# Feed-forward block order, later settling of the down projection, and attention multiplies on VectorE in a hybrid encoder layer

## The chip, the cores and the metric

The kernel runs on one core of one Trainium2 chip. The metric is the device time of one execution in microseconds (us); the kernel before has a median of 1443.12 us over three runs (1441.78 to 1444.57).

## What is computed

One layer on x of 1024 positions by 1024 channels, float32. Cut to what matters here:

```python
h = rmsnorm(x, norm_mix_pre)
conv_in, q, k, v, g_conv, g_att = split(h @ w_in)
u = glu(conv_in); u = causal_depthwise_conv(u, 31 taps); u = silu(layernorm(u))
conv_out = u @ w_conv_branch + b
# stick-breaking attention, 8 heads of 64, strictly causal, in blocks of 128 queries:
#   a[t, s] = sigmoid(z[t, s]) * prod over s < r < t of sigmoid(-z[t, r])
att_out = attention(q, k, v) @ w_att_branch
merged = sigmoid(g_conv) * conv_out + sigmoid(g_att) * att_out
x = x + rmsnorm(merged @ w_out, norm_mix_post)
gate, up = split(rmsnorm(x, norm_ffn_pre) @ w_ffn_up)        # 2 x 2816 columns
x = x + rmsnorm((silu(gate) * up) @ w_ffn_down, norm_ffn_post)
```

## The kernel before, in words

**Precision by halves.** Every matrix is held as a high part (rounded, type float32r) and a low part (what is left). ScalarE copies the high part, and VectorE or GpSimd subtracts it from the source for the low part. A product is three matmuls: high by high, high by low, low by high (`mm3`, L76). A helper `load_w` (L66) loads a weight block, and its subtraction runs on the engine that `low_of` names (L64, GpSimd until L436, then VectorE).

**Who sets the order.** Up to L1103 a scheduler orders each engine's instructions by their place in the program and by when their tiles' slots come free. From L1103 on, each engine keeps the program's order (`Ordered`, L935): what stands first in the program is first in the engine's queue, and a waiting instruction holds what is behind it. SyncE issues all loads and stores of that part in order.

**Start and attention** (L148 to L428). Eight blocks of 128 rows are normalised (`pre`, L166; the scale by the row's root is L177, the root's power is GpSimd's, L107), transposed and split, and v is projected. Then come 8 heads, each in 4 steps of two query blocks. For each block of scores (`chunk`, L237) TensorE makes z, ScalarE the sigmoids of -z and z, VectorE a product scan from the right (L257 for the diagonal part, L262 for a full chunk of 512 columns), and the scan is multiplied by the sigmoid of z: on VectorE for the diagonal part (L259), on GpSimd for a full chunk (L263). `weigh` (L307) transposes the result on TensorE, splits it, and multiplies by v. Projections of later heads and of the conv branch fill TensorE in between; their weights come through `load_w`.

**Output projection** (L683 to L845). For each of 8 row blocks `tb`: `out_steps`, `post` (norm, residual, second norm) and `operands(tb - 2)` (transposes, and the sums that the feed-forward wants). The first two of the eight output weights sit in slots of the pool `wst` that the feed-forward's gate weights (`fetch_gate` L807, `prep_a` L811) use later.

**Feed-forward up** (L943 to L1042). 22 column blocks `f`. Each is a 2 by 2 block product done with seven products instead of eight (numbers 1 to 7, `product` L916), of 12 matmuls each, on operands T1 to T4 and B11, B21, B22 and on sums of the gate and up weights. Products 1 and 2 of blocks 0 to 2 are made early (L839). Within a block, 1 and 2 give u2 and gate1; 6 is added to u2, 7 gives u3, 5 makes up2 and the new u2, then 3 gives the second gate and 4 the first up half. Block 0 is special, since T4 is computed on VectorE in its middle (`make_t4`, L920), and so is the last one, where B22 has to come free. Each product has one of eight PSUM banks. For the next block, `sums_12` and `split_12` make the weights of products 5 and 6, `sums_34` and `split_34` those of 7 and 3, `prep_c` that of 4; `weight_sums` makes sums of the down weights. Activations and their pair sums (`quads`, L1029) go to DRAM by way of the list `late`, which `flush` (L861) empties into SyncE's queue.

**Feed-forward down** (L1056 to L1204). The same seven-product scheme in the order 1, 6, 7, 5, 4, 2, 3 (L1067), each product over 6 steps of two of the 11 column groups (the last step has one): 42 steps in all. `fetch(n)` loads both operands of step n, `ready(n)` splits them (two copies on ScalarE, two subtractions on VectorE, L1083), `cell(n, p, bank)` does piece p of 4, 6 matmuls (3 in the half step that ends each product), and `evacuate(i, p, bank)` takes a finished piece from PSUM (L1156). For products 4 and 2/3 that includes `square` (ScalarE), `gained` (times the gain, on GpSimd or VectorE) and `finish` (L1149: root, then two scaled sums with x1 and the stores). `x1_of` (L1144) loads x1 into one of two buffers. The loop:

```python
for n, (i, gs) in enumerate(work_list):
    fetch(n + AHEAD + 2); flush()
    ready(n + AHEAD)                 # AHEAD = 3
    if i == order[-1]: continue
    for p in range(4):
        cell(n, p, banks[p])
        if gs[-1] == NG - 1: evacuate(i, p, banks[p])
for p in range(4):                   # the last product, piece by piece
    for n in range(N - len(steps), N): cell(n, p, banks[p])
    evacuate(order[-1], p, banks[p]); flush()
```

## Time and profile before

| what | value |
|---|---|
| median of three runs | 1443.12 us (1441.78 to 1444.57) |
| the profiled execution, its own time | 1447.73 us |
| its span, first to last instruction | 1445.9 us |
| TensorE matmuls, busy | 1371.8 us (95%), 6412 |
| VectorE busy | 1044.4 us (72%), 1509 instructions |
| ScalarE busy | 529.2 us (37%) |
| GpSimd busy | 169.8 us (12%) |
| mean granted TensorE clock | 0.983 |

PE is TensorE, PEld its weight loads, DVE VectorE, ACT ScalarE, POOL GpSimd, SPq SyncE's queue. In a timeline a row gives start, duration, engine, line and operation; a bracket at its end says how long the engine sat idle before it and what ended that. From L1103 on all instructions carry the line of the ordering helper, L941, so they are told apart by their tiles: md is a bank of the down projection, m one of the up projection, wl and wh are low and high parts. A matmul's duration overlaps the next one's; what counts is the distance between starts. The granted clock is 1.00 at the upper of the two levels (2.4 GHz) and 0.5 at the lower (1.2 GHz).

### The profile page before, as it was taken

The numbers are of one execution on the slowest core, as the hardware profiler recorded it, in microseconds if no ns is written. First come the engines' busy times: TensorE is split into PE (matmuls) and PEld (weight loads), VectorE is DVE, ScalarE is ACT, GpSimd is POOL, SyncE is SP. The second block draws the span as 40 slices with busy tenths as digits, with TensorE's granted clock in tenths as the row PEclk, the third lists the DMA queues.
The fourth block names the chain that finished last, engine by engine and source line by source line (L and its number), as shares of the span: only waits on it lengthen the run. The fifth ranks groups of instructions, "written<-read, shape, count | busy, mean of one in ns | idle before, by whom it ended". The sixth has DMA issues, their size and how long they took to land.

```text
span 1445.9 us, 17263 instructions
## 1 busy us (share of the span) xinstructions
PE 1371.8 (95%) x6412; PEld 1127.8 (78%) x6412; DVE 1044.4 (72%) x1509; ACT 529.2 (37%) x863; POOL 169.8 (12%) x259
## 2 busy tenths in 40 slices
PE   6988899999999999999997899999999998999987
PEld 5866787777787888888886688888888887888866
DVE  5498887865999967236559889888888775644573
ACT  5466655554111126132335233222222222632350
POOL 2133333331000000000126000000000000000220
PEclk9999999999999999999998999999999999999998
DMA  6011010100102021114322344444444435964272
GB/s 224 23 26 41 9 37 30 45 29 15 51 22 69 27 88 37 51 44 158 126 87 74 124 168 167 167 167 168 157 163 145 147 131 207 374 226 160 103 262 102
DMA packets 62403, 160.97 MB, mean 111 GB/s; under 512 B 6384, under 2 KB 17904, under 8 KB 62320
## 3 DMA queue, kind: packets, MB, share of 16 engines
q1 hardware_dynamic: 62032, 158.83, 32.1%
q8 instruction: 50, 0.82, 0.2%
q10 hardware_dynamic: 288, 1.05, 0.2%
q14 instruction: 33, 0.27, 0.1%
HBM read 117.65 MB, written 40.11 MB: 109 GB/s over the span
## 4 chain that ended last, share of the span: by engine, by line
PE 72%; DVE 18%; issue 3%; ACT 3%; DMA 1%; POOL 1%; SPq 0%; DVEq 0%; POOLq 0%; ACTq 0%
PE m L941 28%; PE md L941 12%; DVE p L469 7%; PE pg L82 3%; PE pg L79 3%; PE pg L80 3%; PE po L697 2%; PE po L695 2%; PE po L696 2%; DVE R L262 2%; PE pb L82 1%; DVE R L257 1%; PE pb L79 1%; PE pb L80 1%; PE av L293 1%
## 5 line engine op out<-in xcount | busy, mean ns | idle before, releaser
L941 PE MATMUL m<-t,wh 128*128 128x512 f32 x528 | 134.9, 397 | 4.4 <-ACT wh L941 3.0
L941 PE MATMUL m<-hH,wh 128*128 128x512 f32 x328 | 130.6, 398 | 8.9 <-ACT wh L803 8.9
L941 PE MATMUL md<-wl,wh 128*128 128x512 f32 x308 | 123.3, 400 | 9.7 <-DVE wl L941 9.7
L941 PE MATMUL m<-hL,wh 128*128 128x512 f32 x328 | 130.1, 397 | 0.0
L941 PEld LDWEIGHTS m<-t,wh 128*128 128x128 f32 x528 | 100.0, 190 | 29.0 <-ACT wh L941 3.4
L941 PE MATMUL md<-wh 128*128 128x512 f32 x308 | 122.4, 398 | 0.0
L941 ACT ACTIVATE c<-c 128x512 f32<-128x512 f32 x44 | 27.9, 634 | 244.9 <-DVE c L941 244.9
L72 ACT ACTIVATE wh<-wraw 128x1024 fp32r<-128x1024 f32 (+1 forms) x60 | 56.5, 946 | 124.7 <-PE pg L80 30.2
L79 PE MATMUL pg<-hH,wh 128*128 128x512 f32 x256 | 100.7, 393 | 0.0
L80 PE MATMUL pg<-hL,wh 128*128 128x512 f32 x256 | 99.7, 389 | 0.0
L941 PE MATMUL md<-wh,wl 128*128 128x512 f32 x308 | 99.3, 397 | 0.0
L941 PE MATMUL m<-hH,wl 128*128 128x512 f32 x328 | 89.2, 393 | 0.0
L73 DVE TENSOR_TENSOR wl<-wraw,wh 128x1024 fp32r<-128x1024 f32 (+1 forms) x45 | 46.7, 1049 | 48.5 <-ACT wh L72 36.7
L941 PEld LDWEIGHTS m<-hH,wh 128*128 128x128 f32 x328 | 62.2, 190 | 23.8 <-ACT wh L803 9.3
L469 DVE SCALAR_TENSOR_TENSOR p<-u,dw,p 128x513 f32<-128x513 f32 (+1 forms) x116 | 80.2, 789 | 0.0
L941 PEld LDWEIGHTS md<-wl,wh 128*128 128x128 f32 x308 | 59.3, 193 | 24.7 <-DVE wl L941 11.8
L941 DVE TENSOR_TENSOR wl<-ra,wh 128x1024 fp32r<-128x1024 f32 (+1 forms) x42 | 48.5, 1154 | 37.9 <-ACT wh L941 37.8
L941 PEld LDWEIGHTS m<-hL,wh 128*128 128x128 f32 x328 | 62.2, 190 | 14.0
L941 PEld LDWEIGHTS m<-hH,wl 128*128 128x128 f32 x328 | 61.7, 188 | 14.4
L941 PE MATMUL m<-t,wl 128*128 128x512 f32 x264 | 70.7, 390 | 0.0
L941 DVE TENSOR_TENSOR u<-m,u 128x512 f32<-128x512 f32 x66 | 45.4, 688 | 33.8 <-PE m L941 32.1
L941 PEld LDWEIGHTS md<-wh 128*128 128x128 f32 x308 | 59.3, 193 | 12.8 <-ACT wh L941 0.3
(235 smaller groups left out, 3326.3 us busy)
## 6 DMA issues: line engine op xcount, KB each, us to landing
ra<-act SPq DMA_DIRECT2D x35, 512.0 KB, 7.1
wraw<-in_wi SPq DMA_DIRECT2D x32, 512.0 KB, 3.5
rg<-in_wu SPq DMA_DIRECT2D x23, 512.0 KB, 4.5
ru<-in_wu SPq DMA_DIRECT2D x22, 512.0 KB, 5.5
q<-in_wdq SPq DMA_DIRECT2D x22, 512.0 KB, 6.3
wsum<-q SPq DMA_DIRECT2D x22, 512.0 KB, 2.6
act<-sa SPq DMA_DIRECT2D x44, 256.0 KB, 2.7
rb<-wsum SPq DMA_DIRECT2D x20, 512.0 KB, 9.6
```

Of the source, the lines that this page charges most:

```text
L72: A.activation(out=wh, in_=raw, func=AF.Copy)
L73: (sub or low_of[0]).tensor_tensor(out=wl, in0=raw, in1=wh.bitcast(F32), op=ALU.subtract)
L79: PE.matmul(ps, lhsT=lh, rhs=rh, start=(first and j == 0), stop=False)
L80: PE.matmul(ps, lhsT=lh, rhs=rl, start=False, stop=False)
L82: PE.matmul(ps, lhsT=ll, rhs=rh, start=False, stop=(last and j == n - 1))
L257: V.tensor_tensor_scan(out=R[:, 3:3 + n][:, ::-1], data0=d, data1=d, initial=1.0, op0=ALU.mult, op1=ALU.bypass)
L262: V.tensor_tensor_scan(out=R[:, 4:4 + n][:, ::-1], data0=d, data1=d, initial=carry, op0=ALU.mult, op1=ALU.bypass)
L469: V.scalar_tensor_tensor(out=to if last is None else last, in0=u[:, k:k + n], scalar=w, in1=to, op0=ALU.mult, op1=ALU.add)
L695: PE.matmul(pb, lhsT=hH[:, d, tsl], rhs=wos[d][0][:, es], start=(d == 0), stop=False)
L696: PE.matmul(pb, lhsT=hL[:, d, tsl], rhs=wos[d][0][:, es], start=False, stop=False)
L697: PE.matmul(pb, lhsT=hH[:, d, tsl], rhs=wos[d][1][:, es], start=False, stop=(d == NK - 1))
L941: return lambda *a, **k: tc.keep_in_program_order(fn(*a, **k))
```

## The change

Seven edits. `low_of` starts with VectorE. The multiply of a full chunk (L263) goes from GpSimd to VectorE. The fetch and split of the gate weights of blocks 0 and 1 stand three row blocks earlier in the program. Block 0 and the last block of the feed-forward up run product 5 before 3; in block 0 all of T4 is made before product 6 and the next block's first sums and split stand right behind it, with the other sums further down; in the last block `ready(0)` stands before product 6. The pair sums of the last block are put off until `ready(1)` has been issued. In the down projection a finished product's pieces are evacuated one step later, behind the next `ready`; product 4's `gained` runs on VectorE and its `finish` one piece later; and the last product runs its pieces 0 and 1 step by step like the other products, pieces 2 and 3 one after the other.

```diff
-    low_of = [G]
+    low_of = [V]
...
-            G.tensor_tensor(out=R[:, 4:4 + n], in0=sg[:, 0:n], in1=R[:, 4:4 + n], op=ALU.mult)
+            V.tensor_tensor(out=R[:, 4:4 + n], in0=sg[:, 0:n], in1=R[:, 4:4 + n], op=ALU.mult)
...
-        if NT - 4 < tb < NT - 1:
-            f = tb - NT + 3
-            fetch_gate(f)
-            prep_a(f)
+        if tb < 4:
+            fetch_gate(tb - 2)
+            prep_a(tb - 2)
...
         if f == 0 or last:
+            run(5)
             run(3)
-            run(5)
             if f == 0:
-                make_t4(range(2))
+                make_t4(range(4))
+            if last:
+                ready(0)
             run(6)
             after_6()
             if f == 0:
-                make_t4(range(2, 4))
+                sums_12(nf)
+                split_12(nf)
...
-        if f == 0:
-            sums_12(nf)
-            split_12(nf)
-            sums_34(nf)
-            weight_sums(f)
-        if last:
-            ready(0)
...
         V.tensor_tensor(out=a2, in0=up2, in1=gate2, op=ALU.mult)
+        if f == 0:
+            sums_34(nf)
...
             prep_c(nf)
+        if f == 0:
+            weight_sums(f)
...
+            def pair_sums():
+                s = {i: half_tile(f"sa{i}", "a", 8) for i in (5, 6, 7, 3)}
...
+            if last:
+                return pair_sums
+            pair_sums()
...
-        up(f)
+        last_sums = up(f)
...
     fetch(1)
     fetch(2)
+    ready(1)
+    last_sums()
     flush()
...
-    for n in range(1, AHEAD):
-        ready(n)
+    ready(2)
...
+    roots = {}
+
+    def root(sst):
+        return power_of(sst[:, 0:1], 1, sst[:, 1:2])
+
-    def finish(tb, parts, sst, xt):
-        r = power_of(sst[:, 0:1], 1, sst[:, 1:2])
+    def finish(tb, parts, r, xt):
...
             square(0, c21[p], sst2[p])
-            gained(0, c21[p], G)
-            finish(p + 4, (c21[p], c22[p]), sst2[p], xt)
+            gained(0, c21[p], V)
+            roots[p] = root(sst2[p]), xt
+            for q in ([p - 1] if p else []) + ([p] if p == 3 else []):
+                finish(q + 4, (c21[q], c22[q]), *roots[q])
...
-    banks = []
+    banks, done = [], []
+
+    def settle():
+        for args in done:
+            evacuate(*args)
+        done.clear()
+
+    FIRST_OF_LAST = N - len(steps)
     for n, (i, gs) in enumerate(work_list):
...
             ready(n + AHEAD)
-        if i == order[-1]:
-            continue
-        for p in range(4):
+        settle()
+        for p in range(4 if n < FIRST_OF_LAST else 2):
             cell(n, p, banks[p])
             if gs[-1] == NG - 1:
-                evacuate(i, p, banks[p])
-    for p in range(4):
-        for n in range(N - len(steps), N):
+                done.append((i, p, banks[p]))
+    for p in (2, 3):
+        for n in range(FIRST_OF_LAST, N):
             cell(n, p, banks[p])
-        evacuate(order[-1], p, banks[p])
+        settle()
         flush()
+        done.append((order[-1], p, banks[p]))
+    settle()
+    flush()
```

## Rows read from the trace of the kernel before

**Rows 1.** Busy time in 20 us stretches: us, engines' busy us (instructions), granted clock, DMA, GB/s
```profile
80.00:100.00 20.00, 15.72 (x93) 12.59 (x93) 19.58 (x34) 12.36 (x28) 8.55 (x19) 1.00 0.00 1
...
740.00:760.00 20.00, 20.00 (x95) 16.37 (x93) 12.88 (x17) 8.82 (x17) 7.73 (x6) 1.00 0.33 107
```

**Rows 2.** Timeline of the start, VectorE and TensorE: start us, us, engine, line, operation
```profile
26.12 3.38 DVE L177 SCALAR_TENSOR_TENSOR xt<-xt,pr,gpre 128x1024 f32<-128x1024 f32 x1 [1.04 <-POOL pr L107]
...
30.89 1.28 DVE L177 SCALAR_TENSOR_TENSOR xt<-xt,pr,gpre 128x1024 f32<-128x1024 f32 x1 [0.73 <-POOL pr L107]
...
29.64 1.06 PE L115 MATMUL tp<-ident,xt 128*128 128x128 f32 x8 [2.64 <-DVE xt L177]
```

**Rows 3.** Groups by line and shape, attention: count, busy us, mean ns, idle before
```profile
L263 POOL TENSOR_TENSOR R<-sg,R 128x512 f32<-128x512 f32 x32 | 46.7, 1461 | 78.2 <-DVE R L262 74.8 <-PE tpa L317 1.8 <-ACT aH L322 1.6
...
L73 POOL TENSOR_TENSOR wl<-wraw,wh 128x1024 fp32r<-128x1024 f32 x15 | 37.0, 2469 | 62.1 <-ACT wh L72 57.5 <-issue 4.6
...
L73 DVE TENSOR_TENSOR wl<-wraw,wh 128x1024 fp32r<-128x1024 f32 x29 | 35.8, 1238 | 48.5 <-ACT wh L72 36.7 <-PE pg L82 11.2 <-issue 0.4
...
L259 DVE TENSOR_TENSOR R<-sg,R 128x511 f32<-128x511 f32 x16 | 14.9, 933 | 0.6
...
L259 DVE TENSOR_TENSOR R<-sg,R 128x255 f32<-128x255 f32 x16 | 13.4, 839 | 0.9
```

**Rows 4.** Timeline, VectorE: the same multiply alone and beside a GpSimd multiply
```profile
65.81 0.42 DVE L259 TENSOR_TENSOR R<-sg,R 128x255 f32<-128x255 f32 x1
...
80.11 1.23 DVE L259 TENSOR_TENSOR R<-sg,R 128x255 f32<-128x255 f32 x1
```

**Rows 5.** Chain that ended last, 60 to 365 us, shares by line (cut short by the view)
```profile
by line: DVE R L262 7.7%; issue 7.1%; DVE R L257 6.2%; PE av L293 5.3%; PE tpa L317 5.3%; DVE aL L323 5.1%; PE av L292 4.8%; PE psg L82 4.2%; DVE R L259 3.7%; PE psg L80 3.7%; PE psg L79 3.5%; PE z L245 3.0%; PE psq L82 3.0%; PE psk L82 2.9
```

**Rows 6.** Timeline of the feed-forward's first block, ScalarE, VectorE and TensorE
```profile
786.50 1.06 ACT L803 ACTIVATE wh<-s 128x1024 fp32r<-128x1024 f32 x1 [1.24 <-DVE s L896]
790.92 1.06 ACT L803 ACTIVATE wh<-rg 128x1024 fp32r<-128x1024 f32 x1 [3.36 <-DVE rg L901]
...
791.41 0.68 DVE L941 TENSOR_TENSOR da<-t,hH 128x512 f32<-128x512 f32 x1
...
792.72 2.76 DVE L941 TENSOR_TENSOR da<-da,db 128x512 f32<-128x512 f32 x1
...
792.03 0.80 PE L941 MATMUL m<-hH,wh 128*128 128x512 f32 x1 [8.86 <-ACT wh L803]
...
812.75 3.65 PE L941 MATMUL m<-t,wh 128*128 128x512 f32 x8 [2.99 <-ACT wh L941]
```

**Rows 7.** Timeline of the output projection's last block, ScalarE
```profile
754.07 2.03 ACT L803 ACTIVATE wh<-rg 128x1024 fp32r<-128x1024 f32 x2
```

**Rows 8.** Timeline of the down projection's start, TensorE, SyncE's queue and ScalarE
```profile
1212.61 0.50 PE L941 MATMUL md<-wl,wh 128*128 128x512 f32 x1 [1.42 <-DVE wl L941]
...
1220.79 0.50 PE L941 MATMUL md<-wl,wh 128*128 128x512 f32 x1 [2.44 <-DVE wl L941]
...
1221.68 0.33 SPq L941 DMA_DIRECT2D rb<-in_wd  x1
...
1228.19 1.06 ACT L941 ACTIVATE wh<-ra 128x1024 fp32r<-128x1024 f32 x1 [10.51 <-DMA ra<-act]
```

**Rows 9.** Timeline of the down projection: first matmul of three products, VectorE near its end
```profile
1246.85 0.40 PE L941 MATMUL md<-wh 128*128 128x512 f32 x1
...
1366.92 0.40 PE L941 MATMUL md<-wh 128*128 128x512 f32 x1
...
1401.44 0.40 PE L941 MATMUL md<-wh 128*128 128x512 f32 x1
...
1384.07 1.22 DVE L941 TENSOR_TENSOR wl<-ra,wh 128x1024 fp32r<-128x1024 f32 x1
...
1438.50 0.69 DVE L941 TENSOR_TENSOR du<-md,du 128x512 f32<-128x512 f32 x1 [3.08 <-PE md L941]
```

**Rows 10.** Waits over the span: who waited for whom: us in total, times, longest
```profile
PE md L941 <- DVE wl L941: 9.7, 5, 2.8
```

More of the change, by code (lines that the diff above doesn't have):

```diff
@@ L1035, in up @@
             keep(4, a22)
-            s = {i: half_tile(f"sa{i}", "a", 8) for i in (5, 6, 7, 3)}
-            V.tensor_tensor(out=s[5], in0=a21, in1=a22, op=ALU.add)
-            V.tensor_tensor(out=s[7], in0=a11, in1=a21, op=ALU.subtract)
-            V.tensor_tensor(out=s[6], in0=s[5], in1=a11, op=ALU.subtract)
-            V.tensor_tensor(out=s[3], in0=a12, in1=s[6], op=ALU.subtract)
-            for i in (5, 7, 6, 3):
-                keep(i, s[i])
+            def pair_sums():
+                s = {i: half_tile(f"sa{i}", "a", 8) for i in (5, 6, 7, 3)}
+                V.tensor_tensor(out=s[5], in0=a21, in1=a22, op=ALU.add)
+                V.tensor_tensor(out=s[7], in0=a11, in1=a21, op=ALU.subtract)
+                V.tensor_tensor(out=s[6], in0=s[5], in1=a11, op=ALU.subtract)
+                V.tensor_tensor(out=s[3], in0=a12, in1=s[6], op=ALU.subtract)
+                for i in (5, 7, 6, 3):
+                    keep(i, s[i])
+            if last:
+                return pair_sums
+            pair_sums()
     with tc.high_priority(300):
@@ L1182, in evacuate @@
             gained(1, c12[p], V)
-            finish(p, (c11[p], c12[p]), sst1[p], xt)
-    banks = []
+            finish(p, (c11[p], c12[p]), root(sst1[p]), xt)
+    banks, done = [], []
[4 more added lines that the diff above has]
+    FIRST_OF_LAST = N - len(steps)
     for n, (i, gs) in enumerate(work_list):
```

## The prediction

> **What bounds the kernel now.** I read the page first: TensorE is busy for nearly the whole span, but the count of matmuls in equal stretches says more than its busy time, because matmuls are pipelined. So the next view was the table of 20 us stretches [rows 1]. The reader is to see two kinds of stretch there: one where VectorE is full and TensorE has holes (80 to 100, inside attention), and one where TensorE is full and everything else has room (740 to 760, output projection). The change puts work on VectorE in the first kind and reorders it around the second, so it has to be costed stage by stage; a share over the whole span would say nothing. After that I went through the timelines of the five places that the diff touches [rows 2, 6 to 9], and the groups of instructions and the chain inside attention [rows 3 to 5].
>
> **The change part by part.** The sum is made against the profiled execution, 1447.73 us, which lies 4.6 us above the median of the three runs, 1443.12. I carry the difference over to the median.
>
> *First weights, on VectorE.* The low parts of the first two attention weights are computed by GpSimd while the normalisation still runs. The scale of a block of x, 1.28 us elsewhere, takes 3.38 us beside the second of them, and TensorE waits 2.64 us for it [rows 2]. The small power that the scale needs also sits behind the first of these subtractions on GpSimd. With both on VectorE the neighbour is gone; VectorE gets two instructions of 1.24 us [rows 3], which can stand in front of the scale in their turn. Bounds: 0 if they do, and -4.4 if the wait goes together with the 1.8 us that the half-speed stretch after it costs (an estimate: 8 matmuls took 3.65 us at the lower level in [rows 6], 1.8 us more than eight at 0.23). I take **-3**.
>
> *Attention, on VectorE.* Added: 32 multiplies of 512 columns at 0.68 us (the price of such an operation on two SBUF tiles [rows 6]), 21.8 us, and 13 further weight parts of 1.24 us, 16.1 us [rows 3]. Removed: what GpSimd did to VectorE. A 255-column multiply takes 0.42 us alone and 1.23 us beside a GpSimd multiply [rows 4]; its 16 average 0.839 us and the 511-column ones 0.933 us [rows 3], so these two forms give back 16 x 0.42 + 16 x 0.25 = 10.7 us. VectorE ends with 37.9 - 10.7 = 27.2 us more. How much of that is on the path? The chain inside attention gives its four named VectorE lines 7.7 + 6.2 + 5.1 + 3.7 = 22.7% [rows 5]; TensorE has the most. 22.7% of 27.2 is 6.2 us. The third form of multiply gives something back too, and the multiply no longer queues on a second engine, so I take **+5**. Bounds: -3 (the shorter way from scan to transpose outweighs the work) and +27.2 (all of it on the path).
>
> The rule that speaks against this edit is in the Trainium skill, Perfetto Trace Analysis, Optimizing Scalar/DVE Operations: a saturated VectorE may be relieved by work given to ScalarE or even GpSimd, and this edit does the reverse. By that rule the stage would cost the upper bound rather than +5; the same passage doubts the relief between VectorE and GpSimd, because they share a read port, and the 1.23 us row agrees with the doubt, though no row shows the saturated case over the whole stage.
>
> *prep_a moved three blocks up.* Its two splits need the slots that hold the first two output weights, and those are read until the last block. The profile has the two copies at 754.07, back to back, long after ScalarE had time for them [rows 7]: the slot sets their time, not their place in the program. TensorE is full at that time [rows 1]. Cost **0**; if the pair now goes in front of a neighbour on ScalarE or GpSimd it moves something by one instruction, which the full TensorE covers.
>
> *First block of the feed-forward.* TensorE waits 8.86 us for the high part of product 3's weight, copied at 790.92; the weight of product 5 is copied at 786.50 [rows 6]. With 5 in front it restarts at 787.6 instead of 792.0, then needs product 3's weight when it is there. The four products 5, 3, 6 and 7 end at about 801.3 (4 x 2.73 us, 1.8 for the lower clock, 1.0 for product 3's low part). Now T4 is late: its 16 VectorE instructions begin at 791.41 at 0.65 us from one to the next, 2.1 us more for the one beside GpSimd that took 2.76, until about 804.0 [rows 6]. The update of u2 queues behind them, and with eight banks taken (four early ones, then 5, 3, 6, 7) product 4 waits for the bank that this update frees: 804.7, a new wait of 3.4 us. The next block's product 6 needs two sums (1.3), a copy (1.06), and a bank freed by u3, which queues behind the low part (1.24 and 0.69): about 809.0, against 812.75 [rows 6]. That is 3.7 us sooner, and up to 1.8 more, as before its first eight matmuls ran at half speed. Blocks 1 and 2 then have less slack on VectorE. I take **-3.3**, bounds 0 (VectorE paces these blocks) and -5.6.
>
> *Last block and start of the down projection.* ready(0) and ready(1) come before other VectorE work, so the waits of 1.42 and 2.44 us go [rows 8], with about 0.8 us of clock. But the fourth step is next: its loads leave SyncE's queue at 1221.68, behind the stores of the pair sums, and ScalarE gets the data at 1228.19 [rows 8]. Two copies (1.06) and two subtractions (1.24) later, about 1231.7, the step can run. TensorE, started at 1210.8 with 24 matmuls of 0.2274 us a step, would be there at 1227.2; before, it came at 1231.8. The pair sums come after the two parts of ready(1), at the same time as before, so their stores and this load do too. The gain is waited away: **0**, bounds -4.7 (the load comes sooner) and +1.8 (a longer idle stretch followed by the lower clock).
>
> *Settling later.* The first cells of products 6 and 2 stand at 1246.85 and 1366.92 [rows 9]: four products without a wait, 30.02 us each. Product 2 takes 34.52, until 1401.44, and product 3 takes 37.06, until its last evacuation at 1438.50. The cause is in VectorE's queue: the parts of step 33 come at 1384.07, behind all of product 4's finishing, and again after product 2's. All waits of TensorE for these parts are 9.7 us [rows 10], of which 3.86 belong to the start, so 5.8 here; the rest is clock. In the new order ready comes before the evacuations and has three steps, 16 us, of lead; finishing product 4 then takes VectorE about 16 us (3.75 a piece with its wait for ScalarE), and the parts it delays are needed a step later than they come. The last product runs its first two pieces step by step, so its late parts are wanted after 10 us and not after 4. 34.52 + 37.06 - 2 x 30.02 = 11.5; I take **-11.3**, bounds -12 and -4.6 (below). The tail after the last evacuation, 7.4 us, keeps its instructions. The multiplies moved from GpSimd to VectorE here and the root drawn forward are within the 16 us.
>
> Sum: -3 + 5 + 0 - 3.3 + 0 - 11.3 = **-12.6 us**, 1435.1 for the profiled execution, **1430.5** for the median.
>
> **The rivals.**
> *SyncE's queue takes the place of VectorE's.* The loads of x1 have two buffers, so the third waits for a finish, and the fetches of the last product queue behind it. For it: those loads share the in-order queue with the fetches. Against it: finishing ends some 3 us sooner than before. If product 3 keeps its waits, 6.9 of the 11.3 us are lost: 1437.4.
> *Attention breaks even.* If the removed contention lies on the path and the added work in VectorE's gaps, attention gives -3 instead of +5: 1422.5. For it, the contended multiplies lie in the stretch where VectorE is full [rows 1, 4]; against it, the same stretch gets the new ones.
> *Attention slower, and the whole slower.* VectorE, in order, becomes the bound from the first to the last head. The price is the 27.2 us; it decides once attention costs over 17.6 us, the sum of the other terms. At the full price: 1443.1 - 17.6 + 27.2 = 1453. Against it: TensorE leads the chain [rows 5].
> *No change that can be measured.* Attention +9 and a fourth step at +1.8 together with a last product that keeps its waits: 1443.1 - 3 + 9 - 3.3 + 1.8 - 4.4 = 1443.2. Nothing in the profile ties these together.
> That the change doesn't do what it says holds for prep_a alone, and is in the sum.
>
> **How the numbers follow.** Forecast 0.57, SyncE's queue 0.15, attention even 0.15, no change 0.06, slower 0.07. About 0.2%, 2.9 us, is what a measurement of this kernel can tell from no change. Faster: 0.57 + 0.15 + 0.15 = 0.87; same 0.06; slower 0.07. The forecast's own range, with attention between -1 and +11, is 1424 to 1437; with the two other faster cases, 1420 to 1440.
>
> **What would show it.** In the profile after: the 3.38 us scale gone and TensorE without a wait before 30 us; no GpSimd product in attention, the 255-column multiply at 0.42 us throughout, and VectorE some 27 us busier there; the first feed-forward product about 4 us after the last early one, then a wait of about 3.4 us before product 4; no wait at the first two steps of the down projection but one of about 4 us at the fourth; no wait from product 2 to the end. I am wrong if attention's length grows by over 12 us, if TensorE still waits for low parts in the last two products, or if the first block's gain is gone two blocks later.

## The result, and the profile after

The kernel after takes **1418.05 us** (median of four runs, 1417.30 to 1418.29); the kernel before 1443.41 (1441.78 to 1444.57). The ratio is 0.9826, 95% interval 0.9814 to 0.9839: 25.4 us faster. The prediction said 1430.5, range 1420 to 1440. The direction was right; the gain is twice the forecast and outside the range.

The profiled execution after took 1417.84 us (span 1416.0). The kernel before was profiled once more (run a0_before): 1442.6 us, against 1447.73 for the execution that the prediction read. Both stand in the table of stages, read from the starts of matmuls that bound each stage:

| stage, us | before | before again | after | forecast | measured |
|---|---|---|---|---|---|
| start, to the first k projection | 48.9 | 50.1 | 45.9 | -3 | -3.1 to -4.2 |
| attention, to the last `av` | 305.3 | 302.4 | 295.7 | +5 | **-6.7 to -9.6** |
| conv branch and output projection, to the first early product | 411.4 | 411.3 | 411.8 | 0 | +0.4 to +0.5 |
| early products, first two feed-forward blocks, three products of the third | 71.1 | 71.5 | 67.9 | -3.3 | -3.1 to -3.6 |
| the rest of the up blocks | 374.2 | 374.2 | 374.2 | 0 | 0 |
| down, first product | 36.1 | 34.4 | 32.6 | 0 | -1.8 to -3.5 |
| down, products 6, 7, 5, 4 | 120.1 | 120.1 | 120.1 | 0 | 0 |
| down, product 2 | 34.5 | 33.1 | 30.0 | } -11.3 | -3.0 to -4.5 |
| down, product 3 and tail | 44.5 | 43.9 | 37.8 | } | -6.1 to -6.7 |

So one row has the wrong sign, and it holds 12 to 15 us; every other is within 3.5 us of its forecast.

**Attention.** The same stretches as in [rows 1], after:

```profile
80.00:100.00 20.00, 18.35 (x105) 14.54 (x105) 19.63 (x36) 12.71 (x28) 2.60 (x15) 1.00 0.00 1
740.00:760.00 20.00, 19.77 (x96) 16.23 (x95) 18.58 (x22) 12.47 (x24) 15.72 (x9) 1.00 0.41 141
```

VectorE was full between 80 and 100 before and still is, but TensorE now does 105 matmuls there instead of 93. The groups of [rows 3] (count, busy us, mean ns, idle before), and the full chunk's scan:

```profile
L263 DVE TENSOR_TENSOR R<-sg,R 128x512 f32<-128x512 f32 x32 | 21.7, 679 | 1.2 <-DVE R L262 0.5
L73 DVE TENSOR_TENSOR wl<-wraw,wh 128x1024 fp32r<-128x1024 f32 x14 | 17.0, 1215 | 8.2 <-PE psg L82 5.8 <-ACT wh L72 1.7 <-PE psq L82 0.7
L259 DVE TENSOR_TENSOR R<-sg,R 128x511 f32<-128x511 f32 x16 | 10.9, 682 | 0.4
...
L259 DVE TENSOR_TENSOR R<-sg,R 128x255 f32<-128x255 f32 x16 | 6.7, 419 | 0.2
...
L262 DVE TENSOR_TENSOR_SCAN R<-qf,R 128x512 f32<-128x512 f32 x32 | 40.8, 1275 | 0.0
```

The multiplies beside GpSimd are back at their price alone, 419 and 682 ns, as forecast. The whole stage, one row each of the table of stretches (start:end, length, then busy us of TensorE, its weight loads, VectorE, ScalarE and GpSimd, granted clock, DMA), the first profiled execution of before, the second, and after:

```profile
48.92:354.17 305.25, 279.74 (x1570) 233.73 (x1568) 232.05 (x380) 169.92 (x347) 97.19 (x175) 0.98 0.10 30
```

```profile
50.05:352.41 302.36, 275.44 (x1569) 229.69 (x1568) 231.86 (x380) 169.64 (x347) 97.07 (x175) 0.99 0.11 30
```

```profile
45.86:341.53 295.67, 276.90 (x1569) 227.04 (x1568) 248.65 (x425) 168.21 (x347) 19.85 (x126) 1.00 0.11 30
```

VectorE is 16.6 us busier, GpSimd 77 us less, the stage is shorter, and the clock is at its upper level throughout. VectorE's idle time went from 73 to 47 us.

**Start.** The 3.38 us scale of [rows 2] is gone, and the matmuls that had waited 2.64 us for it go on without a wait:

```profile
25.62 1.28 DVE L177 SCALAR_TENSOR_TENSOR xt<-xt,pr,gpre 128x1024 f32<-128x1024 f32 x1
...
27.07 1.15 PE L115 MATMUL tp<-ident,xt 128*128 128x128 f32 x8
```

**Feed-forward's first block**, TensorE and VectorE after, to set beside [rows 6]:

```profile
775.35 0.79 PE L940 MATMUL m<-hH,wh 128*128 128x512 f32 x1 [4.40 <-ACT wh L803]
...
792.21 2.48 PE L940 MATMUL m<-t,wh 128*128 128x512 f32 x8 [2.76 <-DVE u L940]
...
791.38 0.68 DVE L940 TENSOR_TENSOR u<-m,u 128x512 f32<-128x512 f32 x1
```

The wait ahead of the first product went from 8.86 to 4.40 us, and 2.76 us of a new wait for `u` stand ahead of product 4 (forecast 3.4). In the kernel before, VectorE itself had waited in this block, between the two halves of T4, for product 6:

```profile
802.34 0.69 DVE L941 TENSOR_TENSOR u<-m,u 128x512 f32<-128x512 f32 x1 [3.54 <-PE m L941]
```

**prep_a.** `741.84` in place of `754.07` [rows 7], 12.2 us earlier like all around it; the edit moved nothing:

```profile
741.84 2.03 ACT L803 ACTIVATE wh<-rg 128x1024 fp32r<-128x1024 f32 x2
```

**Down projection.** Its start (SyncE's queue, ScalarE, TensorE), the first matmuls of the products, and VectorE at the end, to set beside [rows 8, 9]:

```profile
1205.96 0.33 SPq L940 DMA_DIRECT2D rb<-in_wd  x1
...
1211.03 1.06 ACT L940 ACTIVATE wh<-ra 128x1024 fp32r<-128x1024 f32 x1 [10.84 <-DMA ra<-act]
...
1213.09 0.50 PE L940 MATMUL md<-wh 128*128 128x512 f32 x1 [1.10 <-ACT wh L940]
...
1214.54 0.50 PE L940 MATMUL md<-wl,wh 128*128 128x512 f32 x1 [0.95 <-DVE wl L940]
...
1228.05 0.40 PE L940 MATMUL md<-wh 128*128 128x512 f32 x1
...
1348.13 0.40 PE L940 MATMUL md<-wh 128*128 128x512 f32 x1
...
1378.15 0.40 PE L940 MATMUL md<-wh 128*128 128x512 f32 x1
...
1408.57 0.69 DVE L940 TENSOR_TENSOR du<-md,du 128x512 f32<-128x512 f32 x1 [1.14 <-PE md L940]
```

Steps 1 to 3 run without a wait, the fourth waits 1.10 and 0.95 us, and nothing waits afterwards: all waits for low parts, 9.7 us in [rows 10], are now

```profile
PE md L940 <- DVE wl L940: 0.9, 1, 0.9
```

### The profile page after: what moved, and what is told of

The parts are those of the page before. It is cut to its first block, busy times and chain, and to the rows that moved or that the text cites. A ratio compares the mean times of both kernels' runs of the same rounds, so it can differ in the third digit from the quotient of the medians.

```text
span 1416.0 us, 17251 instructions
## 1 busy us (share of the span) xinstructions
PE 1363.2 (96%) x6412; PEld 1116.4 (79%) x6412; DVE 1063.1 (75%) x1560; ACT 527.0 (37%) x863; POOL 87.0 (6%) x208
## 4 chain that ended last, share of the span: by engine, by line
PE 74%; DVE 16%; issue 3%; ACT 3%; DMA 2%; POOL 1%; SPq 0%; DVEq 0%; POOLq 0%; ACTq 0%
PE m L940 26%; PE md L940 13%; PE pg L82 4%; PE pg L80 4%; PE pg L79 4%; PE pb L82 2%; DVE R L262 2%; PE pb L80 2%; PE pb L79 2%; PE psg L82 2%; DVE R L257 2%; PE psg L80 2%; DVE p L469 2%; PE psg L79 2%; DVE aL L323 2%
## 5 line engine op out<-in xcount | busy, mean ns | idle before, releaser
L940 PE MATMUL md<-wl,wh 128*128 128x512 f32 x308 | 120.1, 390 | 0.9 <-DVE wl L940 0.9
L73 DVE TENSOR_TENSOR wl<-wraw,wh 128x1024 fp32r<-128x1024 f32 (+1 forms) x60 | 64.1, 1074 | 57.3 <-ACT wh L72 38.8
L940 ACT ACTIVATE wh<-ra 128x1024 fp32r<-128x1024 f32 (+1 forms) x42 | 41.4, 986 | 84.6 <-PE md L940 56.4
```

The lines of the kernel that those rows point to most:

```text
L73: (sub or low_of[0]).tensor_tensor(out=wl, in0=raw, in1=wh.bitcast(F32), op=ALU.subtract)
L940: return lambda *a, **k: tc.keep_in_program_order(fn(*a, **k))
```

## The experiments

The texts number their theories anew in each group. In a1 to a3, theory 1 is the price of GpSimd (VectorE held up beside it, and a detour from scan to transpose), theory 2 VectorE's added work by its share of the chain, theory 3 GpSimd's weight parts. From d1 on, theory 1 is again the price of GpSimd, and theory 2 the order that the scheduler gives the instructions when an engine assignment changes.

### One edit of attention at a time

**a0_before** is the kernel before, unchanged.

> The kernel before, profiled once more, to find where the 4.6 us lie by which its first profiled execution was over the median. Theory 1 (the excess lies in attention, with the spells at the lower clock): last av about 353 instead of 357.6 after the span's start, the stages behind it as long as before to 0.3 us. Theory 2 (it lies in the last products of the down projection): attention the same 308.6 us from the first psk to the last av, and products 2 and 3 some 4 us shorter than 34.5 and 36.6. Attention's gain by the change is then 9.6 us or 5 us.

Measured: 1442.6 us, attention 302.4 us, products 2 and 3 1.5 and 0.6 us shorter. Both theories hold in part: of the 5.1 us between the two spans, 2.9 lie in attention, 2.1 in products 2 and 3, 1.6 at the start of the down projection, while the start is 1.1 and the first block 0.5 longer. (The text's 357.6 and 308.6 us don't fit the trace: the last `av` starts at 354.17, 305.3 us after the first `psk`.) The clock goes with attention's part: four of its 20 us stretches are at 0.91 or 0.92 in the first execution, one in the second.

**a1_mul**, **a2_low** and **a3_both**:

```diff
-            G.tensor_tensor(out=R[:, 4:4 + n], in0=sg[:, 0:n], in1=R[:, 4:4 + n], op=ALU.mult)
+            V.tensor_tensor(out=R[:, 4:4 + n], in0=sg[:, 0:n], in1=R[:, 4:4 + n], op=ALU.mult)
```

```diff
-    low_of = [G]
+    low_of = [V]
```

> Before with the multiply of a full chunk on VectorE, weight low parts still on GpSimd. Theory 1 (the GpSimd multiply was the price: it held VectorE's two-input operations and stood between scan and transpose): attention 6 to 9 us shorter, total 1434 to 1437. Theory 2 (VectorE's added work is on the path by its share of the chain, 22.7%): 21.8 us added less 10.7 given back, so +2.5, total 1446. Theory 3 (the gain comes from GpSimd's weight parts going away): within 2 us of before.

> Before with all weight low parts on VectorE, the multiply still on GpSimd. All theories: 3 us less before the first psk. Theory 1: attention within 2 us of before, total 1438 to 1442. Theory 2: 16.1 us added at 22.7%, +3.7, total 1444. Theory 3: attention 6 to 9 us shorter, total 1431 to 1434.

> Before with both edits of attention and none of the others. If the stages add: the change's whole gain of 25.4 us less first block 3.1, start of the down projection 3.5 and settling 11.2, so 7.6 us less, total about 1435.5. Theory 1: within 2 us of the multiply alone less the 3 us of the start. Theory 2: the sum of both single edits is far from this value, since VectorE's gaps are used up by the first.

Measured: 1445.92 us (ratio 1.0017, 1.0008 to 1.0026), 1438.04 (0.9959, 0.9947 to 0.9972) and 1432.95 (0.9923, 0.9909 to 0.9936). Attention takes 308.3, 302.5 and 295.7 us. The edits don't add: alone, one costs attention 3 to 6 us and the other changes it by no more than 2.8, together they save 6.7 to 9.6. The totals of a1 and a2 are what theory 2 (1446) and theory 1 (1438 to 1442) had put down, but no theory gives both, and a3 lies 8 us below the lowest that theory 1 allows it. Part of it is visible in a1_mul: the weight parts left on GpSimd are as slow as before and now meet the multiplies, which take 739 ns instead of the 679 of after.

```profile
L73 POOL TENSOR_TENSOR wl<-wraw,wh 128x1024 fp32r<-128x1024 f32 x13 | 32.8, 2523 | 76.5 <-ACT wh L72 64.5 <-PE tpa L317 6.4 <-ACT sg L254 5.6
...
L263 DVE TENSOR_TENSOR R<-sg,R 128x512 f32<-128x512 f32 x32 | 23.7, 739 | 0.9
```

But 32 x 0.06 us is 1.9 us. The rest was looked for in the order, for each of these kernels has one of its own: the scheduler places every instruction of start and attention anew, and between before and after 723 of TensorE's 1,824 instructions there stand at another place in its order. An edit undone alone undoes its order too. So the next runs hold the order.

### Engines and order apart

The order of one built kernel was recorded as a list for each engine and imposed on another by dependencies that only order, without a wait. It holds the instructions that both kernels share, on TensorE, ScalarE, VectorE and SyncE; the multiplies and low parts that differ are put between them by the scheduler. **d1_after_oldorder** is the kernel after in the order of before; **d2_before_neworder** the kernel before in the order of after; **d3_oldorder_pe** the kernel after with TensorE alone in the old order.

```diff
     drain(0)
+    force_order(tc)
     att_ctx.close()
...
+                if prev is not None:
+                    tc.add_manual_dep(i, prev.name, mybir.DependencyInfo(mybir.DependencyClass.NoSync, mybir.DependencyReason.DATA), reason="order")
+                prev = i
```

> The kernel after, in which the instructions of start and attention that both kernels share are held, on TensorE, ScalarE, VectorE and SyncE, in the order in which they stand in the kernel before; the multiplies and low parts on VectorE are put between them by the scheduler. Theory 1 (price: the gain in attention comes from GpSimd's contention and its way round from scan to transpose): attention stays about 296 us from the first psk to the last av, total 1418 to 1421. Theory 2 (order: the gain comes from the new order that the scheduler found): attention about 302 to 305 us, total 1425 to 1428.

> The kernel before, with its multiplies and low parts on GpSimd, in which the shared instructions of start and attention are held in the order of the kernel after. Theory 1 (price): attention 302 to 306 us or longer, total 1443 or more. Theory 2 (order): attention about 296 us, total 1434 to 1437.

> The kernel after, in which TensorE alone is held to the order of the kernel before in start and attention; the scheduler orders the other engines anew around it. With all engines held to the old order attention took 311 us, in the new order 296. Theory 2a (TensorE's order carries it: which projections fill the stretches in which VectorE is full): attention 306 to 311 us, total 1428 to 1436. Theory 2b (VectorE's and ScalarE's order carries it: what stands in front of the scans): attention 296 to 300 us, total 1418 to 1423.

Measured: 1436.20 us (ratio 0.9946, 0.9932 to 0.9961), 1440.79 (0.9980, 0.9971 to 0.9989) and 1435.31 (0.9945, 0.9930 to 0.9961). The attention stage of d1, d2 and d3, one row each:

```profile
48.34:359.44 311.10, 280.11 (x1570) 231.77 (x1568) 249.34 (x425) 169.91 (x347) 19.91 (x126) 0.98 0.10 29
```

```profile
49.43:349.96 300.53, 274.62 (x1569) 227.41 (x1568) 236.80 (x380) 168.00 (x347) 97.39 (x175) 1.00 0.11 30
```

```profile
46.63:363.21 316.58, 282.38 (x1570) 233.78 (x1568) 250.26 (x425) 169.35 (x347) 20.21 (x126) 0.97 0.10 28
```

| attention, us (granted clock) | old order | new order |
|---|---|---|
| multiplies and low parts on GpSimd | 305.3 (0.98), 302.4 (0.99) | 300.5 (1.00) |
| on VectorE | 311.1 (0.98) | 295.7 (1.00) |

In the old order the edit costs 5.9 to 8.7 us, near the +5 of the prediction. In the new order it saves 4.9. The order itself is worth 15.4 us with the work on VectorE and 1.8 to 4.7 without. Up to some 6 of the 15.4 can be the clock (an estimate from d1's row: 0.02 of 311.1 us); the 5.9 and the 4.9 compare rows at like clocks. The profiled executions of d1 and d3 took 1439.21 and 1441.66 us, 4.9 and 8.2 more than the shortest of their five; even if all of that fell to attention, 306.2 and 308.4 us would be left. Theory 2 holds in d1, by more than it had claimed; d2, at 300.5 us, lies between the two; theory 1 falls as an explanation on its own. With TensorE alone held (d3), attention is at 316.6 us, beyond the 306 to 311 of theory 2a: TensorE's old order is enough to lose the gain. What in that order does it is not shown. One thing that differs is where the projection matmuls stand. Counted in the trace, between the third and the fourth `avt` (L298, the copy of `av` that ends half a head) TensorE had 39 projection matmuls before and takes 20.5 us; after it has 26 and takes 14.6, while the interval ahead of it took up six more and went from 14.4 to 15.9. The clock goes with it: after and d2 are at 1.00 over the whole stage, the profiles in the old order (before twice, d1, d3) at 0.97 to 0.99.

### The price of VectorE work and of GpSimd beside it

**b1_double** and **b2_gdummy** put a second multiply behind each full chunk's, in place in `sg`, on VectorE or on GpSimd, and hold the order of after.

```diff
             V.tensor_tensor(out=R[:, 4:4 + n], in0=sg[:, 0:n], in1=R[:, 4:4 + n], op=ALU.mult)
+            extra.append(V.tensor_tensor(out=sg[:, 0:n], in0=sg[:, 0:n], in1=q[:, 1:n + 1], op=ALU.mult).ins.name)
```

> The kernel after with every full chunk's multiply followed by a second one of the same size on VectorE, whose result nothing reads (32 x 0.68 us, 21.8 us more), every other instruction in the order of the kernel after. The price that the prediction used (share of VectorE's lines in the chain, 22.7%): +5, total 1423. Room (VectorE's gaps take it): within 2 us, 1418 to 1420. VectorE is the bound (it is busy 57 to 58 us of 60 between 60 and 180): most of the 21.8 us, 1433 to 1440.

> The kernel after with every full chunk's multiply followed by one of the same size on GpSimd, whose result nothing reads, every other instruction in the order of the kernel after: GpSimd works beside VectorE again, but nothing waits for it. Theory 1 with the price in the contention: VectorE's two-input multiplies at 0.84 and 0.93 us again, about 10 us more VectorE time, total 1422 to 1428. Theory 1 with the price in the way round (scan, GpSimd, transpose): within 2 us of after. Theory 2 (order): within 2 us of after.

Measured: 1453.19 and 1457.24 us, beyond every expectation. The waits of TensorE say why the pair is no measure of what it was meant for (b1_double; in b2_gdummy the same wait is 24.6 us):

```profile
PE z L246 <- ACT sg L255: 21.6, 16, 3.1
```

In after the waits of z for a sigmoid are 1.1 us in all. The extra operation holds `sg` and `qf`, so ScalarE's sigmoids and with them the banks of z come late. Two further runs hold no buffer: **b3_again** does the multiply a second time in place in `R`, right behind the first (the chunk's weights are multiplied twice by the sigmoid), and **b4_gbeside** lets GpSimd do two multiplies of 190 columns into a tile of its own.

```diff
-            V.tensor_tensor(out=R[:, 4:4 + n], in0=sg[:, 0:n], in1=R[:, 4:4 + n], op=ALU.mult)
+            first = V.tensor_tensor(out=R[:, 4:4 + n], in0=sg[:, 0:n], in1=R[:, 4:4 + n], op=ALU.mult)
+            extra[first.ins.name] = [V.tensor_tensor(out=R[:, 4:4 + n], in0=sg[:, 0:n], in1=R[:, 4:4 + n], op=ALU.mult).ins.name]
```

```diff
+            extra[first.ins.name] = [
+                G.tensor_tensor(out=scr, in0=R[:, 4 + o:4 + o + 190], in1=hL[:, 0, o:o + 190].bitcast(F32), op=ALU.mult).ins.name
+                for o in (0, 256)
+            ]
```

> The kernel after, every instruction in its own order, with the multiply of a full chunk done a second time in place right behind the first (the chunk's weights are then multiplied twice by the sigmoid): 32 x 0.68 us, 21.8 us more VectorE work on the way from scan to transpose, no other buffer held. Price by the share of the chain, 22.7%: +5, total 1423. VectorE is what paces attention in this order (272.0 us busy of 295.7): +15 to +22, total 1433 to 1440. Room: within 2 us.

> The kernel after, every instruction in its own order, with two GpSimd multiplies of 190 columns behind the multiply of each full chunk, into a tile of their own that nothing reads: 64 of them, GpSimd beside VectorE and nothing waiting for it. If the neighbourhood alone has a price: VectorE's 255- and 511-column multiplies above 0.42 and 0.68 us, VectorE 5 to 10 us busier in attention, total 1423 to 1430. If not: within 2 us of after.

Measured: 1438.54 us (ratio 0.9957, 0.9944 to 0.9969) and 1423.52 (0.9854, 0.9840 to 0.9869). Their attention rows:

```profile
45.10:359.71 314.61, 280.45 (x1570) 229.38 (x1568) 270.25 (x457) 168.52 (x347) 19.85 (x126) 0.99 0.10 29
```

```profile
45.01:346.05 301.04, 278.12 (x1569) 228.40 (x1568) 253.94 (x425) 168.23 (x347) 74.93 (x190) 0.99 0.11 30
```

b3: VectorE 21.6 us busier, attention 18.9 longer, 88% of the work (these multiplies lie on the way from scan to transpose; of the 18.9 us up to 3 can be the clock, an estimate from 0.99 over 314.61 us). That is what the text gives for a VectorE that paces attention, +15 to +22, though VectorE's busy time in after is 248.65 us and not its 272.0. b4: VectorE 5.3 us busier, attention 5.4 longer (up to 3 of it the clock, in the same way), though nothing waits for GpSimd's result. The neighbourhood has a price, but not where it was expected: VectorE's 255- and 511-column multiplies stay at 419 and 682 ns, and the full chunk's scan takes 1381 ns instead of the 1275 of after:

```profile
L264 DVE TENSOR_TENSOR_SCAN R<-qf,R 128x512 f32<-128x512 f32 x32 | 44.2, 1381 | 0.0
```

The Trainium skill, SBUF — State Buffer, SBUF: two separate sides, says that a GpSimd operation that reads SBUF and a VectorE operation with two SBUF inputs contend for one port pair, which the first of them holds to its end. The scan reads two SBUF inputs, and its row agrees; the 255- and 511-column multiplies read two as well, and theirs show nothing of it in b4.

### The down projection

**c1_nosettle** evacuates at once, **c5_finish** undoes the late finish and the gain on VectorE, **c4_settle_finish** does both.

```diff
-                done.append((i, p, banks[p]))
+                evacuate(i, p, banks[p])
```

```diff
-            gained(0, c21[p], V)
-            roots[p] = root(sst2[p]), xt
-            for q in ([p - 1] if p else []) + ([p] if p == 3 else []):
-                finish(q + 4, (c21[q], c22[q]), *roots[q])
+            gained(0, c21[p], G)
+            finish(p + 4, (c21[p], c22[p]), root(sst2[p]), xt)
```

> The kernel after, with each finished piece of the down projection evacuated right behind its last cell, as before, in place of one step later. Theory: the late evacuation alone carries the term of 11.2 us in products 2 and 3, total 1427 to 1429.5, with TensorE waiting for low parts in product 2 and in the last product. Rival: what carries it is that the last product runs its first two pieces step by step and that finishing is spread over pieces, total within 4 us of after.

> The kernel after, with product 4 finished piece by piece at once and its gain multiplied on GpSimd, as before; the late evacuation stays. If the piece-late finish carries the term (VectorE no longer waits for GpSimd and ScalarE in the middle of its queue): product 2 at 33 to 34.5 us instead of 30.0, total 1421 to 1424. If either of the two edits is enough: within 1 us of after.

> The kernel after, with both undone: pieces evacuated at once, product 4 finished piece by piece with GpSimd. What is left of the settling edits is that the last product runs its first two pieces step by step. If the two edits cover for each other: product 2 at 33 to 34.5 us, product 3 1.8 us or more over after, total 1423 to 1426; the rest of the 11.2 us then belongs to the last product's order of pieces.

Measured: 1419.80 us (ratio 0.9838, 0.9823 to 0.9853), 1419.77 (0.9828, 0.9811 to 0.9845) and 1422.61 (0.9850, 0.9830 to 0.9869). Product 2 takes 30.0, 30.0 and 34.5 us; product 3, to its last matmul, 1.8 us more than in after, 0.9 more and the same. So c1 comes out as its rival had it, c5 between its two cases, and c4 as expected in product 2 but not in product 3. The two edits cover for each other: with both undone the splits of the next step stand behind product 4's last finish on VectorE, which waits for GpSimd's root, and TensorE waits for them:

```profile
1363.82 0.75 DVE L940 SCALAR_TENSOR_TENSOR du<-du,pr,x1r 128x512 f32<-128x512 f32 x1 [1.68 <-POOL pr L940]
...
1365.15 1.22 DVE L940 TENSOR_TENSOR wl<-ra,wh 128x1024 fp32r<-128x1024 f32 x1
...
1367.56 0.80 PE L940 MATMUL md<-wl,wh 128*128 128x512 f32 x1 [2.76 <-DVE wl L940]
```

So product 2's term is settled: 4.4 of its 4.5 us are back, 2.76 of them as the wait. Product 3's 6.1 to 6.7 us come back with neither. In these two products c4 differs from before only in running the last product's first two pieces step by step, and product 3 takes 30.0 us there, to its last matmul, against 36.6 and 36.0 in the two profiles of before: that edit carries the term.

**c2_nostart** puts the pair sums back ahead of the second step's split.

```diff
-            if last:
-                return pair_sums
             pair_sums()
...
-    ready(1)
-    last_sums()
     flush()
...
-    ready(2)
+    for n in range(1, AHEAD):
+        ready(n)
```

> The kernel after, with the pair sums of the last block in their old place and the second step's split behind them. Theory: putting them off carries the 3.45 us at the start of the down projection, total 1421 to 1422, the load of the fourth step coming as late as before and TensorE waiting for low parts at the first steps. The prediction's reason (the fourth step waits the gain away): within 1 us of after, 1418 to 1419.

Measured: 1418.97 us (ratio 0.9834, 0.9819 to 0.9849), within 1 us of after, as the prediction's reason has it. In the trace the second step waits 1.98 us again, and the fourth, which waits 2.05 in after, waits no more.

```profile
1204.00 0.50 PE L940 MATMUL md<-wl,wh 128*128 128x512 f32 x1 [1.98 <-DVE wl L940]
```

The first product takes 33.9 us instead of 32.6, but that is no price of the edit. Its rows in after, in c2 and in f1 (below), which has the edit:

```profile
1195.45:1228.05 32.60, 30.55 (x134) 24.69 (x132) 21.65 (x24) 15.63 (x17) 0.00 (x0) 1.00 0.80 285
```

```profile
1196.15:1230.07 33.92, 31.94 (x134) 25.83 (x133) 23.70 (x26) 18.10 (x21) 0.00 (x0) 0.95 0.88 309
```

```profile
1192.93:1227.20 34.27, 32.15 (x133) 25.85 (x132) 22.65 (x25) 17.04 (x19) 0.00 (x0) 0.95 0.83 293
```

At a granted clock of 0.95 the product is longer with the edit too, and (1 - 0.95) x 33.92 = 1.7 us (an estimate) covers the 1.3. The putting off is worth nothing that shows. The 1.8 us between the second profile of before (34.4 us, at 1.00) and after is left to the other edits of the last block, the earlier `ready(0)` among them, which were not undone.

### Feed-forward's first block

**c3_35** runs product 3 ahead of 5 in the first block, **c6_sums** moves the second block's sums back, and **f1_lows** is a further change: the low parts of the first block's sums on VectorE.

```diff
-            run(5)
-            run(3)
+            for i in ((3, 5) if f == 0 else (5, 3)):
+                run(i)
```

```diff
-            if f == 0:
-                sums_12(nf)
-                split_12(nf)
...
         V.tensor_tensor(out=u2, in0=ps[5], in1=u2, op=ALU.add)
+        if f == 0:
+            sums_12(nf)
+            split_12(nf)
```

```diff
+    lows[0] = V
     with tc.high_priority(300):
         fetch_up(0)
```

> The kernel after, with product 3 ahead of product 5 again in the first block alone. Theory: the order carries the block's 3.1 us, since product 3's weight is ready 4.4 us after product 5's: total 1421 to 1422.5, TensorE waiting some 8.9 us ahead of the first product. Rival: T4 and the sums, moved at the same time, carry it: within 1 us of after, 1418 to 1419.

> The kernel after, with the second block's first sums and split moved back behind the update of u2 by product 5. If they carry the first block's gain: TensorE waits about 3 us for the weight of the second block's product 6, as before, 3 to 3.6 us longer, total 1421 to 1422. If T4 in one piece carries it: within 1 us of after.

> The kernel after, with the low parts of the first block's sums on VectorE instead of GpSimd. In after, VectorE works without a gap from 771 to 793 us there, and the four operations beside GpSimd's three low parts take 1.64, 1.65, 2.85 and 2.77 us instead of 0.69: 6.2 us. Gone for 0.69 + 2 x 1.23 = 3.2 us of low parts: 3 us less on VectorE. If VectorE paces the block: total 1414.5 to 1416. If the low parts, queued on VectorE in front of T4, come later than before: within 1 us of after, or up to 2 us more.

Measured: 1418.09 us (ratio 0.9831, 0.9816 to 0.9845), 1419.05 (0.9840, 0.9827 to 0.9854) and 1416.39 (0.9821, 0.9808 to 0.9834). In c3 the first wait is 8.83 us again, and the 2.76 us ahead of product 4 are gone; 0.69 us stand ahead of the next block's first product (0.17 in after), which begins 43.2 us after the first early product, as in after:

```profile
780.03 0.80 PE L940 MATMUL m<-hH,wh 128*128 128x512 f32 x1 [8.83 <-ACT wh L803]
...
796.79 2.06 PE L940 MATMUL m<-t,wh 128*128 128x512 f32 x8 [0.69 <-DVE u L940]
```

c6 too ends the row of the table as after does, within 0.1 us. Neither the product order nor the early sums carry the 3.1 us, and both rivals hold. What both keep is T4 in one piece, and with it goes the 3.54 us that VectorE stood idle at 802.34 before: VectorE paces the block. It was not undone alone, nor were the other sums, moved further down, so this is by elimination. f1 tests the reason from the other side. Three of VectorE's operations beside GpSimd's low parts, after and in f1 (the same `s`, second sum and T4 sum; after first):

```profile
772.57 1.64 DVE L895 TENSOR_TENSOR s<-s,rg 128x512 f32<-128x512 f32 x1
...
775.81 2.85 DVE L900 TENSOR_TENSOR rg<-rg,s 128x512 f32<-128x512 f32 x1
...
780.50 2.77 DVE L940 TENSOR_TENSOR da<-da,db 128x512 f32<-128x512 f32 x1
```

```profile
774.13 0.68 DVE L895 TENSOR_TENSOR s<-s,rg 128x512 f32<-128x512 f32 x1
...
777.07 0.68 DVE L900 TENSOR_TENSOR rg<-rg,s 128x512 f32<-128x512 f32 x1
...
780.02 0.68 DVE L940 TENSOR_TENSOR da<-da,db 128x512 f32<-128x512 f32 x1
```

The row of the table is 2.5 us shorter than after's (65.4 against 67.9), near VectorE's balance (3 us). In the profiled execution 1.7 of that go again in the down projection's first product, at the lower clock shown above. In total f1 is the fastest kernel measured, but its ratio lies within the interval of after's, and 1.7 us are less than the 0.2% that can be told apart: the gain is shown for the block, not for the whole.

## Why the prediction was wrong, and where it was right

**First weights, -3:** right, -3.1 to -4.2, and for the reason given: a2, which moves the low parts alone, has the first k projection at 46.1 us, a1, which doesn't, at 49.1. But d1, with the low parts on VectorE and the old order, has it at 48.3: the order has a part in this term too.

**Attention, +5: the step that failed.** The prediction took 27.2 us of added VectorE work and "22.7% of 27.2". The work was less: 16.6 us of busy time, in part since scans and the 383-column multiplies gave something back too. The share was no price. In the old order the edit costs 5.9 to 8.7 us, so that the +5 was near for what it costed, the edit in the order as it stood, but by luck: the work is 17.3 to 17.5 us there and the share 34 to 50%, one set too high and the other too low. In the new order 88% of work added between scan and transpose lands on the path (b3). What is missing from the sum is the order. The text ahead of the prediction says that a scheduler orders start and attention; the prediction then priced the edit as though that order stayed. It did not, and the new one gave 15.4 us (d1 against after, part of it the clock). The lower bound of -3 had no room for it either.

The rule that the prediction weighed, from the Trainium skill (Perfetto Trace Analysis, Optimizing Scalar/DVE Operations), is borne out in the part on the shared port: in b4 VectorE is 5.3 us busier beside GpSimd work for which nothing waits. Its other part, that work may be taken off a full VectorE, fits the old order, where the move to VectorE cost time, and not the new one, where it saved 4.9 us.

**The rival "attention breaks even"** named the right sign with the wrong reason. It put the gain into the removed contention, 1422.5; b4 puts that contention at no more than 5.4 us, with 56.6 us of GpSimd work against the 77 that went.

**prep_a, 0:** right [rows 7].

**First block, -3.3:** right in size, -3.1 to -3.6, and in the 2.76 us wait for the bank that `u2` frees. Its account led with product 5 ahead of 3. That restart came as written (4.40 instead of 8.86 us) and is worth nothing, since T4 on VectorE sets the end (c3).

**Start of the down projection, 0:** off by 1.8 to 3.5 us, within its bounds; of the 3.5, up to 1.8 is the clock, 0.95 in the first profile of before (36.05 us) and 1.00 in after. That the putting off of the pair sums is waited away at the fourth step is borne out (c2). The fourth step was the one that waits, as said, but for 2.05 us and not "about 4". Its data are with ScalarE 15.6 us after the first matmul of the projection (1211.03 - 1195.45), where the prediction carried over the 17.4 of before; and the step starts when its high parts are there, at 1213.09, while the low parts are still to come.

**Settling, -11.3:** -9.1 to -11.2, right in its place, VectorE's queue, and in the wait gone from product 2 on. That late evacuation carries it is too much: for product 2 either edit is enough (c4), and product 3 hangs on the order of its pieces (c4 against before). SyncE's queue did not take the place of the wait.

## What to carry to other kernels

Where a scheduler orders a stage, moving an instruction to another engine changes two things, its price and the order of everything around it; price the second by a range of its own (here 1.8 to 15.4 us of a 300 us stage, some of it the clock) and test it by imposing one kernel's order on the other. An experiment that undoes one edit in such a stage does not isolate it. The share of an engine in the chain of waits says what is on the path now, not what a microsecond more on that engine will cost: in this stage it said 23%, and 34 to 50% (old order: 5.9 to 8.7 us for 17.3 to 17.5 us of VectorE) or 88% (new order, next to the scan) was measured.

## What was not expected of the hardware

d2 and after ran the whole of attention at the upper clock level, with 25.3 and 18.1 us of TensorE waits in all; before, with 24.8 us, had 20 us stretches at 0.91. The sum of the waits does not tell which kernel loses its clock. And GpSimd beside VectorE did not always slow the same operations: the 255-column multiplies before (839 ns on average), the scans in b4 (1381 instead of 1275), the first block's sums (2.85 instead of 0.68).
